# The norm's row scale laid into the third plain tile of each FFN of a one-layer decoder block

## The chip, the cores and the metric

The kernel runs on one core of one Trainium2 chip. The metric is the device time of one execution in microseconds (us); the median of 3 runs is 1043.48 us, the lowest 1042.58 and the highest 1044.74. Engine names are those of the profile: PE does the matmuls and PEld their weight loads, DVE and ACT the elementwise work, POOL hardly anything here, SP issues the loads from HBM.

## What is computed

One layer of a decoder for 512 tokens of width 1024, in float32. The change touches the two feed-forward halves (FFN), which stand before and after the mixing part:

```python
def rms_norm(x, g):
    xf = x.astype(jnp.float32)
    y = xf * lax.rsqrt(jnp.mean(xf * xf, axis=-1, keepdims=True) + EPS)
    return (y * g.astype(jnp.float32)).astype(x.dtype)

def swiglu(x, w_gate, w_up, w_down):
    return (jax.nn.silu(x @ w_gate) * (x @ w_up)) @ w_down
...
        h = h + 0.5 * swiglu(rms_norm(h, ln_ffn1[i]), w1_gate[i], w1_up[i], w1_down[i])
        u = rms_norm(h, ln_mix[i]) @ w_in[i]
...
        h = h + 0.5 * swiglu(rms_norm(h, ln_ffn2[i]), w2_gate[i], w2_up[i], w2_down[i])
```

D_MODEL is 1024 and D_FF is 2816, so one FFN has 22 column tiles of 128.

## The kernel before

The activations lie transposed: `h[k]` holds 128 features by 512 tokens, for 8 values of `k`. Every float32 factor is split into a high and a low part, and one product is three matmuls (`mm3`, lines 228 to 230: high by high, high by low, low by high), each 128 x 128 by 512 columns. The norm's row scale (one number per token) isn't applied to the input. The matmuls run on `h` times the gain, and the scale `rb`, which is the same for all features, multiplies the results as they leave PSUM. So the first tiles can be computed before the scale is known, but none can leave PSUM.

`WStream` delivers the weights: SP loads blocks of 128 x 1024 (`wraw`, 512 KB, 7 buffers), ACT makes the high part (`whi`, line 73) and DVE the low part (`wlo`, line 74), with 3 buffers each, up to 3 pieces ahead of PE. A piece is 8 blocks of 128 x 128, that is 24 matmuls. A `whi` buffer is written again when PE has read it for the last time.

In an FFN, `f` counts the column tiles; each has a gate bank `g` (PSUM pool "acc", 3 banks) and an up bank `u` (pool "t", 3 banks), and takes two pieces, 48 matmuls. Tiles 0 and 1 are computed together (`first`, 96 matmuls), then tile 2 (`plain_pair(2)`, the "third plain tile"), and with it all three pairs of banks are full. Then comes the row scale:

- `norm.finish()`: `col_sums` sums the squares over the features by 4 matmuls against a column of ones (line 268, PSUM tile `ss`), and `rsqrt_of` takes the inverse root by 12 small DVE operations of 128 x 4 (lines 247 to 261);
- `row_bcast`: DVE makes a diagonal matrix in a high and a low part (`dg`, lines 275 and 280), PE multiplies them with ones (lines 282 and 283, PSUM tile `rbp`), and ACT copies the result to `rb` (line 346).

`plain_out` empties a tile: DVE `gs = g * rb` (line 368, frees `g`), ACT `silu(gs)` (line 369, which needs its function table loaded), DVE `a = u * gs` (line 371, frees `u`), and the split of `a` (lines 235 and 236). Tile 3 can start when tile 0's `g` is free. After the plain tiles (6 in the first FFN, 4 in the second) the other tiles are computed as Strassen products of 256 columns (`start_pair`, `end_pair`), whose operands `sx` are formed from `h` by ACT and DVE (`Norm.forms`, lines 316 to 320 and 235, 236; the intermediate is `sf`) and from the weights by DVE (`T1` to `T4`, lines 101 to 110, which write `wraw`). Then comes the down projection.

The program isn't run in the order in which it is written: a scheduler sets each engine's queue, by the dependencies and by when it takes operands to be ready, and each engine then works through its queue in order. So the operand forms of tiles far ahead stand between the operations of the row scale, and the order on the engines has to be read from the queues, below.

## Time and profile before

| | |
|---|---|
| median of 3 runs | 1043.48 us (1042.58 to 1044.74) |
| the profiled execution | 1042.88 us |
| its span, first to last instruction | 1041.1 us |
| PE busy | 1016.6 us, 98% of the span |
| DVE busy | 729.3 us, 70% |
| ACT busy | 449.2 us, 43% |
| PE share of the chain that ended last | 96% |
| mean granted clock of PE | 0.987 of full speed |

The span is the profiled execution without what lies before its first and behind its last instruction (1.8 us here). The time of an engine is the sum of its instructions; matmuls overlap, so a matmul that lasts 0.39 us is followed by the next after 0.23 us when PE is dense. The granted clock tells how much of the 2.4 GHz PE was given: 1.00 is 2.4 GHz, 0.50 is 1.2 GHz. A wait is the idle time of an engine before an instruction, put down to what ended it.

### The profile page before, as it was taken

What the parts mean: (1) busy time and instruction counts of PE and PEld (TensorE: products, weight loads), DVE (VectorE), ACT (ScalarE), POOL (GpSimd) and SP (SyncE); (2) the same over time, 40 slices, a digit from 0 to 9 for tenths busy, and PEclk for the clock granted to TensorE, in tenths of its full rate; (3) what the DMA queues carried; (4) which work ended last, traced back from release to release, by engine and by line L of the source; (5) the groups of instructions that cost most, each with busy time, mean ns of one, the idle gap of its engine ahead of it and who ended that gap; (6) DMA issues with size and microseconds to landing.
All of it is one profiled execution on the core that took longest, in us unless ns stands there. A gap on an engine that the chain in (4) does not pass through costs nothing.

```text
span 1041.1 us, 14828 instructions
## 1 busy us (share of the span) xinstructions
PE 1016.6 (98%) x5987; PEld 886.6 (85%) x5987; DVE 729.3 (70%) x1181; ACT 449.2 (43%) x692; POOL 2.5 (0%) x9
## 2 busy tenths in 40 slices
PE   9799999999999999999999998899999999999996
PEld 7689998899998888887767787799988999988885
DVE  7857975579976668765647676688744698866655
ACT  8334552145544342345443442455522255543443
POOL 0000000000000000000000000000000000000000
PEclk9899999999999999999999999899999999999998
DMA  8212253123343221122210222033333132342301
GB/s 326 61 61 82 82 173 108 61 82 102 111 151 123 92 92 61 51 82 92 72 60 1 82 82 81 5 113 121 122 107 101 61 102 82 133 151 101 101 21 61
DMA packets 28980, 97.68 MB, mean 94 GB/s; under 512 B 3456, under 2 KB 3456, under 8 KB 28912
## 3 DMA queue, kind: packets, MB, share of 16 engines
q1 hardware_dynamic: 28752, 96.25, 27.4%
q8 instruction: 47, 0.77, 0.3%
q0 software_dynamic: 160, 0.49, 0.2%
q14 instruction: 21, 0.17, 0.0%
HBM read 94.10 MB, written 2.10 MB: 92 GB/s over the span
## 4 chain that ended last, share of the span: by engine, by line
PE 96%; DVE 2%; DMA 1%; issue 0%; ACT 0%; SPq 0%; DVEq 0%
PE down L228 8%; PE down L229 8%; PE down L230 8%; PE a L384 6%; PE a L383 6%; PE a L382 6%; PE gu L228 4%; PE gu L229 4%; PE gu L230 4%; PE c L382 3%; PE c L384 3%; PE c L383 3%; PE b L384 2%; PE b L382 2%; PE b L383 2%; PE ufq L228 2%
## 5 line engine op out<-in xcount | busy, mean ns | idle before, releaser
L73 ACT ACTIVATE whi<-wraw 128x1024 fp32r<-128x1024 f32 (+1 forms) x220 | 230.1, 1046 | 394.9 <-PE down L229 94.6
L74 DVE TENSOR_TENSOR wlo<-wraw,whi 128x1024 fp32r<-128x1024 f32 (+1 forms) x220 | 265.1, 1205 | 91.8 <-ACT whi L73 91.0
L228 PE MATMUL down<-ah,whi 128*128 128x512 f32 x352 | 137.1, 390 | 0.0
L229 PE MATMUL down<-al,whi 128*128 128x512 f32 x352 | 137.1, 390 | 0.0
L230 PE MATMUL down<-ah,wlo 128*128 128x512 f32 x352 | 137.0, 389 | 0.0
L382 PE MATMUL c<-sx,whi 128*128 128x256 f32 x272 | 78.7, 289 | 0.9 <-DVE u L416 0.9
L228 PEld LDWEIGHTS down<-ah,whi 128*128 128x128 f32 x352 | 66.1, 188 | 14.1 <-ACT ah L235 0.7
L230 PEld LDWEIGHTS down<-ah,wlo 128*128 128x128 f32 x352 | 66.1, 188 | 13.8
L229 PEld LDWEIGHTS down<-al,whi 128*128 128x128 f32 x352 | 66.1, 188 | 13.7 <-DVE al L236 0.4
L384 PE MATMUL a<-x,wlo 128*128 128x256 f32 x272 | 77.0, 283 | 0.0
L384 PE MATMUL a<-sx,wlo 128*128 128x256 f32 x272 | 77.0, 283 | 0.0
L383 PE MATMUL a<-sx,whi 128*128 128x256 f32 x272 | 77.0, 283 | 0.0
L383 PE MATMUL a<-x,whi 128*128 128x256 f32 x272 | 77.0, 283 | 0.0
L382 PE MATMUL a<-sx,whi 128*128 128x256 f32 x272 | 77.0, 283 | 0.0
L384 PE MATMUL c<-sx,wlo 128*128 128x256 f32 x272 | 77.0, 283 | 0.0
L383 PE MATMUL c<-sx,whi 128*128 128x256 f32 x272 | 76.9, 283 | 0.0
L382 PE MATMUL a<-x,whi 128*128 128x256 f32 x272 | 76.9, 283 | 0.0
L228 PE MATMUL gu<-x,whi 128*128 128x512 f32 x160 | 64.5, 405 | 3.0 <-DVE gs L368 2.8
L229 PE MATMUL gu<-x,whi 128*128 128x512 f32 x160 | 63.9, 401 | 0.0
L230 PE MATMUL gu<-x,wlo 128*128 128x512 f32 x160 | 63.5, 398 | 0.0
L382 PEld LDWEIGHTS c<-sx,whi 128*128 128x128 f32 x272 | 52.1, 191 | 3.5 <-DVE u L416 2.9
L382 PEld LDWEIGHTS a<-sx,whi 128*128 128x128 f32 x272 | 52.2, 192 | 0.1
(306 smaller groups left out, 2173.4 us busy)
## 6 DMA issues: line engine op xcount, KB each, us to landing
wraw<-wst SPq DMA_DIRECT2D x169, 512.0 KB, 3.4
h<-xT SPq DMA_DIRECT2D x8, 256.0 KB, 6.4
out<-y SPq DMA_DIRECT2D x8, 256.0 KB, 2.2
wraw<-wst SPq DMA_DIRECT2D x7, 256.0 KB, 2.6
rpb<-rpa SPq DMA_DIRECT2D x8, 64.0 KB, 2.1
praw<-pT SPq DMA_DIRECT2D x2, 256.0 KB, 3.3
gf<-lnf SPq DMA_DIRECT2D x2, 256.0 KB, 4.3
posi<-pos POOLq DMA_DIRECT2D x1, 256.0 KB, 4.4
```

The lines of the kernel that those rows point to most:

```text
L73: self.nc.scalar.activation(hi, src, AF.Copy)
L74: self.nc.vector.tensor_tensor(lo, src, hi.bitcast(F32), op=ALU.subtract)
L228: PE.matmul(out, a[0], b[0], start=start, stop=False)
L229: PE.matmul(out, a[0], b[1], start=False, stop=False)
L230: PE.matmul(out, a[1], b[0], start=False, stop=stop)
L382: PE.matmul(o, hi[:, c], x[0], start=begin and i == 0 and k == 0, stop=False, skip_group_check=True)
L383: PE.matmul(o, hi[:, c], x[1], start=False, stop=False, skip_group_check=True)
L384: PE.matmul(o, lo[:, c], x[0], start=False, stop=end and i == 1 and k == 3, skip_group_check=True)
```

## The change

The tile's loop becomes a generator that can stop after every second `k`. The column sums are issued in front of tile 2, then a one-element Silu (whose result nobody reads), then three quarters of tile 2 (36 matmuls), then `row_bcast`, then the last quarter. The later plain tiles run as before (`next(plain_tile())` runs all 8 `k`). No operation is left out; two Silu of 128 x 1 are added, one for each FFN.

```diff
--- before.py
+++ after.py
@@ -447,20 +447,27 @@
                     mm3(u, W.next(), norm.x(k), k == MO[0], k == MO[-1])
         g, u = acc("gu"), tps("gu")
 
-        def plain_pair(f):
-            for k in MO:
+        def plain_tile(n=KD):
+
+            for i, k in enumerate(MO):
                 for o in (g, u):
                     mm3(o, W.next(), norm.x(k), k == MO[0], k == MO[-1])
-
-        plain_pair(2)
+                if i % n == n - 1:
+                    yield
+
+        tile2 = plain_tile(2)
         r = norm.finish()
+        S.activation(warm, ones, AF.Silu)
+        for _ in range(3):
+            next(tile2)
         rb = row_bcast(r, "rb")
+        next(tile2)
         for f in range(2):
             plain_out(f, first[2 * f], first[2 * f + 1])
         forms = list(range(4))
         for f in range(2, 2 * n_plain):
             if f > 2:
-                plain_pair(f)
+                next(plain_tile())
             if forms:
                 norm.forms(forms.pop(0))
             if n_plain == 2:
```

What stands in the queues now, at the places on which the prediction rests. Lines up to 449 keep their numbers, those behind the changed piece are 7 higher after. Names carry running numbers: `gu_22` and `gu_23` are `g` and `u` of tile 2 in the first FFN, `gu_51` and `gu_52` those of tile 3, `whi5` and `whi6` tile 2's two pieces.

PE in the first FFN before, from the end of tile 2 to the start of tile 3:

```order
L228 MATMUL gu_23_292<-x_13_253,whi6_301 128x512
L229 MATMUL gu_23_292<-x_13_253,whi6_301 128x512
L230 MATMUL gu_23_292<-x_13_253,wlo6_302 128x512
L268 MATMUL ss_24_365<-ones_96,ssum_14_268 128x1 x4
L282 MATMUL rbp_31_393<-dg_29_386,ones_r_98 128x512
L283 MATMUL rbp_31_393<-dg_30_387,ones_r_98 128x512
L228 MATMUL gu_51_440<-x_6_126,whi7_307 128x512
L229 MATMUL gu_51_440<-x_6_126,whi7_307 128x512
```

PE there after, at the end of tiles 0 and 1 (`gu_5` is tile 1's `u`):

```order
L228 MATMUL gu_5_125<-x_13_253,whi4_237 128x512
L229 MATMUL gu_5_125<-x_13_253,whi4_237 128x512
L230 MATMUL gu_5_125<-x_13_253,wlo4_238 128x512
L268 MATMUL ss_24_293<-ones_96,ssum_14_268 128x1 x4
L228 MATMUL gu_22_291<-x_6_126,whi5_317 128x512
L229 MATMUL gu_22_291<-x_6_126,whi5_317 128x512
L230 MATMUL gu_22_291<-x_6_126,wlo5_318 128x512
```

and further on, from the 38th matmul of tile 2 nearly to its end:

```order
L229 MATMUL gu_22_291<-x_12_232,whi6_323 128x512
L282 MATMUL rbp_31_382<-dg_29_375,ones_r_98 128x512
L230 MATMUL gu_22_291<-x_12_232,wlo6_324 128x512
L228 MATMUL gu_23_292<-x_12_232,whi6_323 128x512
L229 MATMUL gu_23_292<-x_12_232,whi6_323 128x512
L230 MATMUL gu_23_292<-x_12_232,wlo6_324 128x512
L228 MATMUL gu_22_291<-x_13_253,whi6_323 128x512
L229 MATMUL gu_22_291<-x_13_253,whi6_323 128x512
L230 MATMUL gu_22_291<-x_13_253,wlo6_324 128x512
L228 MATMUL gu_23_292<-x_13_253,whi6_323 128x512
L229 MATMUL gu_23_292<-x_13_253,whi6_323 128x512
L283 MATMUL rbp_31_382<-dg_30_376,ones_r_98 128x512
```

The column sums went ahead of tile 2's 48 matmuls; the two broadcast matmuls went into it, the first behind 38 of them and the second behind 47, so that one matmul is left behind it before tile 3. In tile 3 the 12 matmuls of its first half that write `g` still stand ahead of those that write `u`.

DVE in the first FFN before, from the last operand forms to the gate of tile 0 (the rows left out between the two pieces are five more small operations of the inverse root):

```order
L101 TENSOR_TENSOR wraw15_618<-wraw13_614,wraw14_616 128x1024
L319 SCALAR_TENSOR_TENSOR sf_78_677<-h3_74,vec_70,a21_77_676 128x256
L320 SCALAR_TENSOR_TENSOR sf_78_677<-h7_78,vec_70,sf_78_677 128x256
L247 TENSOR_SCALAR rv_25_370<-ss_24_365 128x4
L250 TENSOR_SCALAR ry_26_372<-rv_25_370 128x4
L251 TENSOR_SCALAR ry_26_372<-ry_26_372 128x4
L254 SCALAR_TENSOR_TENSOR rg_28_376<-ry_26_372,rv_25_370 128x4
L256 TENSOR_TENSOR ru_27_375<-rg_28_376,ry_26_372 128x4
L74 TENSOR_TENSOR wlo9_445<-wraw9_442,whi9_444 128x1024
```

```order
L256 TENSOR_TENSOR ru_27_375<-rg_28_376,ry_26_372 128x4
L257 SCALAR_TENSOR_TENSOR ry_26_372<-ru_27_375,ry_26_372 128x4
L275 TENSOR_TENSOR dg_29_386<-ident_112,ry_26_372 128x512
L280 SCALAR_TENSOR_TENSOR dg_30_387<-ident_112,ry_26_372,dg_29_386 128x128 x4
L368 TENSOR_TENSOR gs_33_398<-gu_2_122,rb_32_396 128x512
```

DVE there after, the start of the row scale:

```order
L236 TENSOR_TENSOR sx_56_511<-sf_54_504,sx_55_510 128x512
L247 TENSOR_SCALAR rv_25_298<-ss_24_293 128x4
L250 TENSOR_SCALAR ry_26_300<-rv_25_298 128x4
L74 TENSOR_TENSOR wlo7_330<-wraw7_327,whi7_329 128x1024
L251 TENSOR_SCALAR ry_26_300<-ry_26_300 128x4
L236 TENSOR_TENSOR sx_58_515<-sf_54_504,sx_57_514 128x512
L254 SCALAR_TENSOR_TENSOR rg_28_304<-ry_26_300,rv_25_298 128x4
L317 SCALAR_TENSOR_TENSOR sf_66_590<-h6_77,vec_70,a21_65_589 128x256
L256 TENSOR_TENSOR ru_27_303<-rg_28_304,ry_26_300 128x4
L319 SCALAR_TENSOR_TENSOR sf_66_590<-h2_73,vec_70,a21_65_589 128x256
L257 SCALAR_TENSOR_TENSOR ry_26_300<-ru_27_303,ry_26_300 128x4
L259 SCALAR_TENSOR_TENSOR rg_28_304<-ru_27_303,rg_28_304 128x4
```

and its end, up to the gate of tile 0:

```order
L236 TENSOR_TENSOR sx_70_601<-sf_66_590,sx_69_600 128x512
L257 SCALAR_TENSOR_TENSOR ry_26_300<-ru_27_303,ry_26_300 128x4
L317 SCALAR_TENSOR_TENSOR sf_78_678<-h7_78,vec_70,a21_77_677 128x256
L74 TENSOR_TENSOR wlo8_360<-wraw8_357,whi8_359 128x1024
L275 TENSOR_TENSOR dg_29_375<-ident_112,ry_26_300 128x512
L101 TENSOR_TENSOR wraw15_619<-wraw13_615,wraw14_617 128x1024
L280 SCALAR_TENSOR_TENSOR dg_30_376<-ident_112,ry_26_300,dg_29_375 128x128 x4
L318 SCALAR_TENSOR_TENSOR sf_78_678<-h3_74,vneg_120,sf_78_678 128x256
L319 SCALAR_TENSOR_TENSOR sf_78_678<-h3_74,vec_70,a21_77_677 128x256
L320 SCALAR_TENSOR_TENSOR sf_78_678<-h7_78,vec_70,sf_78_678 128x256
L74 TENSOR_TENSOR wlo9_446<-wraw9_443,whi9_445 128x1024
L368 TENSOR_TENSOR gs_33_399<-gu_2_122,rb_32_385 128x512
```

The small operations of the inverse root, which stood in a row behind all operand forms, now stand one by one between them, and the low diagonal (line 280) comes behind a weight form (line 101); tile 0's gate (line 368) now comes behind `wlo9`, as it did.

PE in the second FFN after, three quarters into tile 2 (`gu_598` and `gu_599` are its `g` and `u`):

```order
L228 MATMUL gu_599_5678<-x_586_5471,whi128_5649 128x512
L229 MATMUL gu_599_5678<-x_586_5471,whi128_5649 128x512
L230 MATMUL gu_599_5678<-x_586_5471,wlo128_5650 128x512
L282 MATMUL rbp_607_5756<-dg_605_5749,ones_r_98 128x512
L283 MATMUL rbp_607_5756<-dg_606_5750,ones_r_98 128x512
L228 MATMUL gu_598_5677<-x_589_5509,whi128_5649 128x512
L229 MATMUL gu_598_5677<-x_589_5509,whi128_5649 128x512
L230 MATMUL gu_598_5677<-x_589_5509,wlo128_5650 128x512
```

DVE in the second FFN before, from the last operand form to the gate of tile 0:

```order
L236 TENSOR_TENSOR sx_646_5919<-sf_642_5908,sx_645_5918 128x512
L107 TENSOR_TENSOR wraw115_5830<-wraw119_5963,wraw115_5830 128x1024
L74 TENSOR_TENSOR wlo129_5681<-wraw113_5678,whi129_5680 128x1024
L74 TENSOR_TENSOR wlo130_5711<-wraw114_5708,whi130_5710 128x1024
L247 TENSOR_SCALAR rv_601_5743<-ss_600_5738 128x4
L250 TENSOR_SCALAR ry_602_5745<-rv_601_5743 128x4
L251 TENSOR_SCALAR ry_602_5745<-ry_602_5745 128x4
L254 SCALAR_TENSOR_TENSOR rg_604_5749<-ry_602_5745,rv_601_5743 128x4
```

DVE there after, the start of the same stretch:

```order
L236 TENSOR_TENSOR sx_646_5921<-sf_642_5910,sx_645_5920 128x512
L247 TENSOR_SCALAR rv_601_5684<-ss_600_5679 128x4
L107 TENSOR_TENSOR wraw115_5832<-wraw119_5965,wraw115_5832 128x1024
L250 TENSOR_SCALAR ry_602_5686<-rv_601_5684 128x4
L74 TENSOR_TENSOR wlo129_5704<-wraw113_5701,whi129_5703 128x1024
L251 TENSOR_SCALAR ry_602_5686<-ry_602_5686 128x4
L254 SCALAR_TENSOR_TENSOR rg_604_5690<-ry_602_5686,rv_601_5684 128x4
L256 TENSOR_TENSOR ru_603_5689<-rg_604_5690,ry_602_5686 128x4
```

and its end:

```order
L257 SCALAR_TENSOR_TENSOR ry_602_5686<-ru_603_5689,ry_602_5686 128x4
L275 TENSOR_TENSOR dg_605_5749<-ident_112,ry_602_5686 128x512
L280 SCALAR_TENSOR_TENSOR dg_606_5750<-ident_112,ry_602_5686,dg_605_5749 128x128 x4
L74 TENSOR_TENSOR wlo130_5734<-wraw114_5731,whi130_5733 128x1024
L368 TENSOR_TENSOR gs_609_5773<-gu_594_5553,rb_608_5759 128x512
```

Here both broadcast matmuls stand behind 36 of tile 2's 48, with 12 behind them. On DVE the inverse root went ahead of `wlo130` and `wlo131`, and a weight form that waits for a load (line 107) stands between its first two operations.

ACT at the start of the program, after:

```order
L213 ACT_TABLE_LOAD
L213 ACTIVATE warm_110<-ones_96 128x1
L460 ACTIVATE warm_110<-ones_96 128x1 x2
L543 ACT_TABLE_LOAD
L543 ACTIVATE lbe0_1533<-lbe0_1533 128x4
L238 ACTIVATE x_6_126<-h0_71,vec_70 128x512
```

Both added Silu (line 460) stand here and not at the FFNs, since they need nothing but `ones`: in both FFNs the order on ACT is still `rb`, table load, `gs`, as in this piece of the second FFN after:

```order
L73 ACTIVATE whi129_5703<-wraw113_5701 128x1024
L73 ACTIVATE whi130_5733<-wraw114_5731 128x1024
L346 ACTIVATE rb_608_5759<-rbp_607_5756 128x512
L369 ACT_TABLE_LOAD
L369 ACTIVATE gs_609_5773<-gs_609_5773 128x512
L73 ACTIVATE whi131_5838<-wraw117_5836 128x1024
```

There `whi131`, which stood ahead of `rb`, went behind the first Silu. The order of the loads on SP and of the work on POOL is the same in both kernels.

## Rows read from the trace of the kernel before

**Rows 1.** The page: busy us, share, instructions; the chain that ended last.
```profile
PE 1016.6 (98%) x5987; PEld 886.6 (85%) x5987; DVE 729.3 (70%) x1181; ACT 449.2 (43%) x692; POOL 2.5 (0%) x9
...
PE 96%; DVE 2%; DMA 1%; issue 0%; ACT 0%; SPq 0%; DVEq 0%
```

**Rows 2.** Who PE waited for: total us, times, longest us.
```profile
PE rbp L282 <- DVE dg L275: 9.4, 2, 5.2
PE gu L228 <- DVE gs L368: 2.8, 2, 1.4
```

**Rows 3.** Timeline of PE, first FFN: start, duration, instruction, [idle before].
```profile
28.34 0.39 PE L228 MATMUL gu<-x,whi 128*128 128x512 f32 x1
...
39.22 0.95 PE L268 MATMUL ss<-ones,ssum 128*128 128x1 f32 x8
44.39 0.77 PE L282 MATMUL rbp<-dg,ones_r 128*128 128x512 f32 x1 [4.22 <-DVE dg L275]
...
47.68 0.79 PE L228 MATMUL gu<-x,whi 128*128 128x512 f32 x1 [1.41 <-DVE gs L368]
...
52.42 0.39 PE L228 MATMUL gu<-x,whi 128*128 128x512 f32 x1
```

**Rows 4.** Timeline of DVE, first FFN.
```profile
29.63 0.69 DVE L236 TENSOR_TENSOR sx<-sf,sx 128x512 fp32r<-128x512 f32 x1 [0.24 <-ACT sx L235]
30.58 1.23 DVE L74 TENSOR_TENSOR wlo<-wraw,whi 128x1024 fp32r<-128x1024 f32 x1 [0.26 <-ACT whi L73]
31.72 0.69 DVE L236 TENSOR_TENSOR sx<-sf,sx 128x512 fp32r<-128x512 f32 x1
32.44 0.48 DVE L317 SCALAR_TENSOR_TENSOR sf<-h,vec,a 128x256 f32<-128x256 f32 x1
...
41.01 0.16 DVE L256 TENSOR_TENSOR ru<-rg,ry 128x4 f32<-128x4 f32 x1
41.09 1.23 DVE L74 TENSOR_TENSOR wlo<-wraw,whi 128x1024 fp32r<-128x1024 f32 x1
...
42.50 0.16 DVE L256 TENSOR_TENSOR ru<-rg,ry 128x4 f32<-128x4 f32 x1
42.70 0.16 DVE L257 SCALAR_TENSOR_TENSOR ry<-ru,ry 128x4 f32<-128x4 f32 x1
...
43.55 0.69 DVE L275 TENSOR_TENSOR dg<-ident,ry 128x512 fp32r<-128x512 f32 x1
44.28 1.14 DVE L280 SCALAR_TENSOR_TENSOR dg<-ident,ry,dg 128x128 fp32r<-128x128 f32 x4
46.93 0.69 DVE L368 TENSOR_TENSOR gs<-gu,rb 128x512 f32<-128x512 f32 x1 [1.51 <-ACT rb L346]
```

**Rows 5.** Timeline of ACT, first FFN.
```profile
39.24 1.06 ACT L73 ACTIVATE whi<-wraw 128x1024 fp32r<-128x1024 f32 x1 [3.39 <-issue]
46.30 0.60 ACT L346 ACTIVATE rb<-rbp 128x512 f32<-128x512 f32 x1 [6.00 <-PE rbp L283]
46.92 1.28 ACT L369 ACT_TABLE_LOAD   x1
48.21 0.63 ACT L369 ACTIVATE gs<-gs 128x512 f32<-128x512 f32 x1
```

**Rows 6.** Timeline of PE, second FFN.
```profile
646.05 0.95 PE L268 MATMUL ss<-ones,ssum 128*128 128x1 f32 x8
655.44 0.80 PE L228 MATMUL gu<-x,whi 128*128 128x512 f32 x1 [1.41 <-DVE gs L368]
...
659.40 0.40 PE L228 MATMUL gu<-x,whi 128*128 128x512 f32 x1
```

**Rows 7.** Timeline of DVE, second FFN.
```profile
636.00 1.23 DVE L107 TENSOR_TENSOR wraw<-wraw,wraw 128x1024 f32<-128x1024 f32 x1 [2.20 <-DMA wraw<-wst]
```

**Rows 8.** Windows: length; PE, PEld, DVE, ACT, POOL busy; granted clock; DMA.
```profile
41.50:42.00 0.50, 0.00 (x0) 0.00 (x0) 0.50 (x1) 0.00 (x0) 0.00 (x0) 0.53 0.00 0
```

**Rows 9.** Timeline of ACT, start of the program.
```profile
4.04 0.72 ACT L238 ACTIVATE x<-h,vec 128x512 fp32r<-128x512 f32 x1 [0.29 <-DMA h<-xT]
```

## The prediction, made before the changed kernel was run

> **What bounds the kernel now.** I read the page first: PE is busy for 98% of the span and is 96% of the chain that ended last [rows 1], so a change counts by what it does to PE's idle time and to PE's clock. Next, whom PE waited for: nearly all of it is two waits, 9.4 us in total for the diagonal `dg` and 2.8 us for tile 0's gate, each twice, that is once in each FFN [rows 2]. Then the timelines of the two places. In the first FFN PE ends tile 2, does the column sums at 39.22, stands idle for 4.22 us until `dg` is there, does the two broadcasts, waits 1.41 us more for the gate and starts tile 3 at 47.68 [rows 3]; in the second FFN the sums start at 646.05 and tile 3 at 655.44 [rows 6]. What fills that time is one chain: sums, inverse root, diagonal (DVE), broadcast (PE), copy (ACT), gate (DVE) [rows 3 to 5]. Last the clock: in the first FFN PE's clock fell in the window from 41.5 us, during the idle time [rows 8], to half, and came back only during tile 3. At full clock a matmul of 512 columns takes 0.227 us (48 of tile 2 from 28.34 to 39.22 are 10.88) [rows 3]; tile 3's first 13 took 4.74 us, from 47.68 to 52.42, and not 2.95, which is 1.8 us lost. In the second FFN the first 9 took 3.96, from 655.44 to 659.40, and not 2.04: 1.9 us lost [rows 6].
>
> **Moved: the sums.** They take 0.95 us before and after [rows 3, 6]; they stand ahead of tile 2 and not behind it. Nothing gained by itself. What is queued behind them is tile 2, and the squares that they wait for are summed long before (the operand forms that follow these sums on DVE are under way at 29.63 [rows 4]).
>
> **First FFN, the inverse root and the diagonal.** The sums now run from 28.34 to 29.29. DVE's first small operation follows the `sx` of 29.63, at 30.25. Up to the high diagonal DVE has 12 small operations and, between them, two `wlo`, three `sx` and five `sf` that belong to later tiles. An operation overlaps the next by 0.09 (30.58 + 1.23 against 31.72), so a `wlo` costs 1.14, an `sx` 0.60, an `sf` 0.40 [rows 4]: 2.28 + 1.80 + 2.00 = 6.1 us. A small operation costs 0.20 where the next one needs its result (42.50 to 42.70) and 0.08 where it doesn't (41.01 to 41.09) [rows 4]; in the new order only two of the twelve are followed at once by one that needs them, so 2 x 0.20 + 10 x 0.08 = 1.2. With 0.1 for the wait of the first `wlo` for its high part (30.58) the high diagonal starts at 30.25 + 6.1 + 1.2 + 0.1 = 37.65 and ends at 38.34. Its broadcast starts 0.15 later, as at 43.55 + 0.69 against 44.39 [rows 3, 4]: 38.5. PE gets there after 38 matmuls, at 29.29 + 8.62 = 37.9. So PE waits 0.6 us in the middle of tile 2, a new wait, with the last ten matmuls behind it. The low diagonal follows a weight form of 1.14 and takes 1.14 itself [rows 4]: 40.55. PE needs it after the broadcast and 9 matmuls, at 38.5 + 2.27 = 40.76. No wait.
>
> **First FFN, what is late next.** ACT has to make `whi9` before it copies `rb`, and `whi9` needs the buffer that PE reads until the 47th matmul, which starts at 40.53 and ends 0.39 later, at 40.92 [rows 3]. It starts 0.08 later, as at 39.24 [rows 5], and `rb` 0.97 after that, at 42.0; with 0.63 from `rb` to the gate (46.30 to 46.93 [rows 4, 5]) the gate could start at 42.6. But `wlo9` stands ahead of it on DVE, waits for `whi9` and runs from 42.1 to 43.24. The gate takes 0.75 until PE starts (46.93 to 47.68 [rows 3, 4]): tile 3 starts at 43.99, after 2.6 us of idle PE, against 47.68: **3.7 us gained**. If each small operation costs 0.20 all of it shifts by 1.2 and 2.5 are gained; without the 0.6 us wait 4.3 are.
>
> **The clock there.** No row of before shows a single idle time of PE between 1.4 and 4.2 us. The lower bound of the loss is none; the upper is what tile 3 lost before, 1.8 us. I take the upper one: the clock fell at 41.5 at the earliest 1.3 us after PE had stopped at 40.17 [rows 3, 8], half of the idle time that I expect. So the 1.8 us stay as they are and none is gained.
>
> **Second FFN.** Tile 2 started at 646.05 - 10.88 = 635.17, so the sums now end at 636.12. On DVE the first small operation runs, then line 107, which waited for a load until 636.00 [rows 7] and is ready; with 1.14 for it and 1.14 for `wlo129`, then ten small operations in a row at 0.20 or less, the high diagonal starts at 640.5, and the low one ends at 640.5 + 0.73 + 1.14 = 642.4 [rows 4]. PE gets to the broadcasts after 36 matmuls, at 636.12 + 8.16 = 644.3, so 1.9 us are to spare. `rb` is copied from 645.0 to 645.6 and the gate ends at 646.3; PE has two broadcasts and 12 matmuls left, 14 x 0.227 = 3.2, and ends tile 2 at 647.5. So tile 3 starts without a wait, at 647.5 against 655.44, 8.0 us, and with no idle time the 1.9 us of slow clock go too: **9.9 us gained**.
>
> **The second bank.** Tile 3's `u` needs the Silu. The added Silu of the change stand at the head of ACT's queue, so each FFN still loads the table behind `rb`. In the rows the load of 1.28 us is followed at once by the Silu, 46.92 to 48.21 [rows 5]. With 0.63 for it and 0.69 for `a`, `u` is free 3.3 us after `rb` starts: at 45.3 in the first FFN, where PE asks for it 13 matmuls into tile 3 at 46.9, and at 648.3 in the second, 7 matmuls in, at 649.1. No wait, by 1.6 and 0.8 us. The Trainium skill (ScalarE: Activation LUTs, "What ACT_TABLE_LOAD costs") puts a drain of about 1.38 us behind each load; the rows have none, and by the page the second FFN would wait 0.6 us.
>
> **Added and not on the path.** The two Silu of 128 x 1 at the start cost 0.2 us each; ACT had 0.29 us idle there before its first `x` [rows 9], so 0.15 us is left, which I add in full. The loads on SP keep their order, and by the time that PE runs ahead the loads of the next pieces have landed: DVE's and ACT's waits there are for PE. I cost them at nothing; if that cover fails, PE waits for DVE's weight forms.
>
> **The sum.** 3.7 + 9.9 - 0.15 = 13.45 us off 1042.88 is 1029.4 for an execution like the profiled one. The median lies 0.6 above that one: **1030.0**.
>
> **Rivals.**
> - *The clock holds in the first FFN.* Then 1.8 us more, 1028.2. For it: 2.6 us idle is less than the 4.2 us that showed the fall. Chance 0.30.
> - *The first FFN only trades its wait.* If the forms between the small operations run later than their durations say (they wait for ACT's `sx`, as at 29.63), PE stands in the middle of tile 2 for what it stood for behind it. Gain of the first FFN 0 to 2.5: 1031.2 to 1033.7. Chance 0.12.
> - *The table load drains.* If the Silu starts later than the rows show, as by the page above, 0.6 us in the second FFN: 1030.6. The rows speak against it. Chance 0.05.
> - *Given back later.* PE arrives 9.9 us earlier at the Strassen products, and DVE has to empty three tiles and make the weight forms for them in the time of tile 3. Three times four operations of 0.60, three `wlo` and two forms of 1.14 are 12.9 us, against 10.9 of tile 3 and 3.2 of the last quarter: it just fits. ACT's Silu between them could stretch it; what doesn't fit comes back as waits for weight forms, at worst in both FFNs and all of it: 1030 to 1043. Chance 0.05, of which 0.03 within 0.2%.
> - *Slower.* In the second FFN line 107 stands ahead of the inverse root and waits for a load; it already waited 2.20 us [rows 7]. Each us that the load is late beyond the 1.9 to spare stops PE in tile 2 for 1 us. From 13.45 + 1.9 = 15.4 us late the kernel is slower; at 20 us it would take 1048. Nothing in the rows has a load that late. Chance 0.02.
> - *The change doesn't do what it says.* That is so for the table load and is in the sum; a hoisted load would have brought nothing, since PE doesn't wait for `u`.
>
> **Chances and range.** The forecast has 0.46. The range 1027.0 to 1033.0 holds it, the clock that holds with 1 us of error, the page's rule and most of the traded wait, about 0.85. A measurement can tell about 0.2% of this kernel, 2.1 us, from no change. Faster by more: 0.95; within: 0.03; slower: 0.02.
>
> **What would show it.** Right: in the second FFN no wait of PE from tile 2 to tile 3 and a granted clock of 1.00 throughout; in the first a wait before the first broadcast of about 0.6 us and one of about 2.6 us before tile 3, put down to the gate, with `wlo9` just ahead of the gate on DVE; a table load behind `rb` in both. Wrong: a wait before the broadcasts in the second FFN, a wait for `u` inside tile 3, or new waits of PE in the products behind the plain tiles.

## The result, and the profile after

The changed kernel takes 1028.76 us, the median of 4 runs (1027.57 to 1029.40), against 1043.84 for the kernel before, timed beside it (4 runs): a ratio of 0.9855, with a 95% interval of 0.9838 to 0.9872. The profiled execution took 1029.4 us, of which 1027.6 are its span. The forecast was 1030.0, and 1029.4 for a profiled execution.

The page of the changed kernel, to be read against [rows 1]: busy us, share, instructions by engine, then the chain that ended last.

```profile
PE 1011.9 (98%) x5987; PEld 883.5 (86%) x5987; DVE 727.4 (71%) x1181; ACT 449.4 (44%) x694; POOL 2.5 (0%) x9
...
PE 93%; DVE 3%; issue 1%; DMA 1%; ACT 1%; SPq 0%; DVEq 0%; ACTq 0%
```

PE is busy for 4.7 us less with the same number of matmuls. So about a third of the 13.5 us is not idle time of PE. By the rows below, about half of that third is tile 3, which ran at the lower clock for a shorter time in the first FFN (0.28 us) and not at all in the second (1.93 us). The rest is mostly the broadcasts: before, these four matmuls lasted 0.77 to 0.80 us each (the first is in [rows 3]), alone and at the lower clock; now they stand among others, where one matmul follows the next after 0.23 to 0.32 us. Whom PE waited for (total us, times, longest us), against [rows 2]:

```profile
PE gu L228 <- DVE gs L368: 2.6, 1, 2.6
...
PE gu L228 <- ACT whi L73: 0.9, 1, 0.9
PE rbp L282 <- DVE dg L275: 0.4, 1, 0.4
```

The 9.4 us for the diagonal have shrunk to 0.4, and the gate's 2.8 us in two waits are now one wait of 2.6 us. The first FFN shows where these two are. First PE from the start of tile 2 to that of tile 3, against [rows 3] (start, duration, instruction, [idle before]):

```profile
28.20 0.95 PE L268 MATMUL ss<-ones,ssum 128*128 128x1 f32 x8
...
37.53 0.39 PE L229 MATMUL gu<-x,whi 128*128 128x512 f32 x1
38.34 0.47 PE L282 MATMUL rbp<-dg,ones_r 128*128 128x512 f32 x1 [0.42 <-DVE dg L275]
...
40.72 0.39 PE L283 MATMUL rbp<-dg,ones_r 128*128 128x512 f32 x1
...
43.94 0.50 PE L228 MATMUL gu<-x,whi 128*128 128x512 f32 x1 [2.59 <-DVE gs L368]
```

Then DVE in the same stretch, against [rows 4], and ACT, against [rows 5]:

```profile
37.51 0.69 DVE L275 TENSOR_TENSOR dg<-ident,ry 128x512 fp32r<-128x512 f32 x1
38.11 1.22 DVE L101 TENSOR_TENSOR wraw<-wraw,wraw 128x1024 f32<-128x1024 f32 x1
39.25 1.14 DVE L280 SCALAR_TENSOR_TENSOR dg<-ident,ry,dg 128x128 fp32r<-128x128 f32 x4
...
42.06 1.23 DVE L74 TENSOR_TENSOR wlo<-wraw,whi 128x1024 fp32r<-128x1024 f32 x1 [0.49 <-ACT whi L73]
43.20 0.68 DVE L368 TENSOR_TENSOR gs<-gu,rb 128x512 f32<-128x512 f32 x1
44.59 0.69 DVE L371 TENSOR_TENSOR a<-gu,gs 128x512 f32<-128x512 f32 x1 [0.70 <-ACT gs L369]
```

```profile
40.97 1.06 ACT L73 ACTIVATE whi<-wraw 128x1024 fp32r<-128x1024 f32 x1 [4.97 <-issue]
41.94 0.58 ACT L346 ACTIVATE rb<-rbp 128x512 f32<-128x512 f32 x1
42.53 1.28 ACT L369 ACT_TABLE_LOAD   x1
43.92 0.63 ACT L369 ACTIVATE gs<-gs 128x512 f32<-128x512 f32 x1
```

The sums now stand ahead of tile 2, at 28.20. The high diagonal starts at 37.51, PE waits 0.42 us for it in the middle of tile 2 (counted from the end of the matmul of 37.53; the broadcast fell due 0.23 us after that matmul's start, at 37.76, and came 0.58 us later), and the low broadcast at 40.72 waits for nothing. ACT makes `whi9` at 40.97 and copies `rb` only behind it; DVE makes `wlo9` at 42.06, behind a wait for `whi9`, and only then the gate at 43.20. For that PE stands idle for 2.59 us and starts tile 3 at 43.94. The granted clock in windows there (length; PE, PEld, DVE, ACT, POOL busy; granted clock; DMA share, GB/s), against [rows 8]:

```profile
44.00:44.50 0.50, 0.50 (x2) 0.42 (x3) 0.00 (x0) 0.50 (x1) 0.00 (x0) 1.00 0.61 66
45.00:45.50 0.50, 0.50 (x4) 0.36 (x3) 0.50 (x2) 0.19 (x1) 0.00 (x0) 0.82 0.81 311
46.00:46.50 0.50, 0.50 (x3) 0.40 (x2) 0.50 (x1) 0.50 (x1) 0.00 (x0) 0.50 0.51 205
49.00:49.50 0.50, 0.50 (x3) 0.39 (x3) 0.50 (x1) 0.00 (x0) 0.00 (x0) 1.00 0.00 0
```

The clock falls to half, from 2.4 to 1.2 GHz, but not in the idle time: PE ended tile 2 at 43.94 - 2.59 = 41.35 and was back at work at 43.94, and the clock stood at 1.00 until 45.0. It is back at 1.00 in the window at 49.0. In the second FFN, PE and DVE, against [rows 6] and [rows 7]:

```profile
631.83 0.95 PE L268 MATMUL ss<-ones,ssum 128*128 128x1 f32 x8
...
640.95 0.39 PE L282 MATMUL rbp<-dg,ones_r 128*128 128x512 f32 x1
641.18 0.39 PE L283 MATMUL rbp<-dg,ones_r 128*128 128x512 f32 x1
...
644.14 0.39 PE L228 MATMUL gu<-x,whi 128*128 128x512 f32 x1
```

```profile
632.81 0.16 DVE L247 TENSOR_SCALAR rv<-ss 128x4 f32<-128x4 f32 x1 [2.35 <-PE ss L268]
632.89 1.22 DVE L107 TENSOR_TENSOR wraw<-wraw,wraw 128x1024 f32<-128x1024 f32 x1
...
637.08 0.69 DVE L275 TENSOR_TENSOR dg<-ident,ry 128x512 fp32r<-128x512 f32 x1
...
642.24 0.69 DVE L368 TENSOR_TENSOR gs<-gu,rb 128x512 f32<-128x512 f32 x1 [1.67 <-ACT rb L346]
```

No row of PE there has an idle time, the granted clock is 1.00 in every half microsecond from 630 to 662, and line 107, which waited 2.20 us for its load before, waits for nothing. The gate at 642.24 waited for the copy `rb`, and is done 1.2 us before PE, with sums, 48 matmuls and two broadcasts behind it, reaches tile 3 at 644.14.

For the balance I take the gate of tile 3, which waits for that tile's last matmul, as the end of each FFN's plain part. The four rows, the kernel before first (DVE, line 368):

```profile
60.10 0.69 DVE L368 TENSOR_TENSOR gs<-gu,rb 128x512 f32<-128x512 f32 x1 [2.07 <-PE gu L230]
...
667.77 0.69 DVE L368 TENSOR_TENSOR gs<-gu,rb 128x512 f32<-128x512 f32 x1 [0.93 <-PE gu L230]
```

```profile
56.08 0.69 DVE L368 TENSOR_TENSOR gs<-gu,rb 128x512 f32<-128x512 f32 x1 [1.84 <-PE gu L230]
...
654.54 0.69 DVE L368 TENSOR_TENSOR gs<-gu,rb 128x512 f32<-128x512 f32 x1 [0.93 <-PE gu L230]
```

| stretch | before, us | after, us | difference |
|---|---|---|---|
| start of the program to tile 2 (after: the sums ahead of it), first FFN | 28.34 | 28.20 | -0.14 |
| to the gate of tile 3, first FFN | 31.76 | 27.88 | -3.88 |
| to the start of tile 2, second FFN (635.17 before, 631.83 after) | 575.07 | 575.75 | +0.68 |
| to the gate of tile 3, second FFN | 32.60 | 22.71 | -9.89 |
| to the end of the span | 373.33 | 373.06 | -0.27 |
| span | 1041.1 | 1027.6 | -13.5 |

### The profile page after: what moved, and what is told of

Its sections match the earlier page's. It is cut to its first block, busy times and chain, and to the rows that moved or that the text cites. A ratio compares the mean times of both kernels' runs of the same rounds, so it can differ in the third digit from the quotient of the medians.

```text
span 1027.6 us, 14828 instructions
## 1 busy us (share of the span) xinstructions
PE 1011.9 (98%) x5987; PEld 883.5 (86%) x5987; DVE 727.4 (71%) x1181; ACT 449.4 (44%) x694; POOL 2.5 (0%) x9
## 4 chain that ended last, share of the span: by engine, by line
PE 93%; DVE 3%; issue 1%; DMA 1%; ACT 1%; SPq 0%; DVEq 0%; ACTq 0%
PE down L228 8%; PE down L229 8%; PE down L230 8%; PE a L384 6%; PE a L383 6%; PE a L382 6%; PE c L382 3%; PE c L383 3%; PE c L384 3%; PE gu L228 3%; PE gu L230 3%; PE gu L229 3%; PE b L384 2%; PE b L383 2%; PE b L382 2%; PE ufq L228 2%
## 5 line engine op out<-in xcount | busy, mean ns | idle before, releaser
L228 PE MATMUL gu<-x,whi 128*128 128x512 f32 x160 | 63.0, 397 | 3.5 <-DVE gs L368 2.6
L229 PE MATMUL gu<-x,whi 128*128 128x512 f32 x160 | 62.6, 392 | 0.0
```

Of the source, the lines that this page charges most:

```text
L228: PE.matmul(out, a[0], b[0], start=start, stop=False)
L229: PE.matmul(out, a[0], b[1], start=False, stop=False)
```

## Experiments

Each kernel differs from the changed kernel by the diff shown. The two with the change in one FFN, the one with the broadcast behind tile 2 and the one with the table load hoisted ran on one chip beside 9 runs of the kernel before (median 1043.17). The one without the small Silu and the one with the broadcast at half of tile 2 ran on another (7 runs, 1042.94), the other four on a third (9 runs, 1043.14). Ratios are to these.

**The change in the first FFN alone, and in the second alone.** `n_plain` is 3 in the first FFN and 2 in the second; the other FFN keeps the old order.

```diff
-        r = norm.finish()
-        S.activation(warm, ones, AF.Silu)
-        for _ in range(3):
+        early = n_plain == 3
+        for _ in range(0 if early else 4):
             next(tile2)
+        r = norm.finish()
+        if early:
+            S.activation(warm, ones, AF.Silu)
+            for _ in range(3):
+                next(tile2)
         rb = row_bcast(r, "rb")
-        next(tile2)
+        if early:
+            next(tile2)
```

> The change in the first FFN alone; the second FFN as in the kernel before. My theory, that the two FFNs add up and the first one only shortens its wait: tile 3 starts at about 43.9 instead of 47.68, PE still idle about 2.6 us before it, the clock falls in most runs; 3.5 us off the median of before (1043.8), so 1040.3, and about 1.8 less in runs in which the clock holds. In the second FFN the old waits (5.2, 0.3, 1.4 us) stand as before. Rival, that the first FFN's gain is given back in the products behind the plain tiles (0.7 us of it was in the profiled execution of the changed kernel): 1041 to 1043.

> The change in the second FFN alone. My theory: all of its idle time and its slow clock go, 9.9 us, so 1033.9 from 1043.8, with no PE wait between tile 2 and tile 3 of the second FFN and the old waits (4.2, 0.3, 1.4 us) in the first. Rival, that the second FFN's gain needs what the first one moved (loads or operand forms that arrive earlier): less than 8 us, above 1036.

Measured: the first FFN alone 1037.24 us, ratio 0.9947 (0.9934 to 0.9961); the second alone 1032.46 (for it, `early = n_plain == 2`), ratio 0.9900 (0.9887 to 0.9914). The second FFN's part brought 10.7 us, 0.8 more than its term; in its profile the stretch from tile 2 to the gate of tile 3 in that FFN is 22.72 us (635.74 to 658.46), 9.88 less than before, as the term has it. The first FFN's brought 5.9, 2.2 more than its term of 3.7, and its 1037.24 us is met neither by the theory (1040.3, or 1.8 less where the clock holds) nor by the rival (1041 to 1043). Its profiled execution shows where most of that comes from; PE and the gate of tile 3, and the clock where the changed kernel's had fallen:

```profile
37.90 0.47 PE L282 MATMUL rbp<-dg,ones_r 128*128 128x512 f32 x1 [0.41 <-DVE dg L275]
...
43.49 0.50 PE L228 MATMUL gu<-x,whi 128*128 128x512 f32 x1 [2.59 <-DVE gs L368]
```

```profile
54.02 0.69 DVE L368 TENSOR_TENSOR gs<-gu,rb 128x512 f32<-128x512 f32 x1 [1.84 <-PE gu L230]
```

```profile
45.00:45.50 0.50, 0.50 (x4) 0.42 (x3) 0.42 (x1) 0.50 (x2) 0.00 (x0) 1.00 0.77 303
46.00:46.50 0.50, 0.50 (x4) 0.42 (x3) 0.50 (x2) 0.09 (x1) 0.00 (x0) 1.00 0.07 25
```

The wait of 2.59 us is the same to the hundredth, but the clock stood at 1.00 behind it, and from tile 3's start to its gate it took 54.02 - 43.49 = 10.53 us where the changed kernel took 56.08 - 43.94 = 12.14. So one and the same idle time is followed by a fall of the clock in one execution and not in another, and the fall costs 1.6 us. The two parts alone make 16.6 us, both together 15.1 (15.4 in the later four runs); I have no reading that accounts for all of that 1.2 to 1.5 us. The fall of the clock, which comes in some executions and not in others, is of that size, and so is the interval of each of these gains, 1.4 to 1.8 us either way.

**The sums in front, the broadcast behind the whole tile 2.** The other half of the change is undone.

```diff
-        for _ in range(3):
+        for _ in range(4):
             next(tile2)
         rb = row_bcast(r, "rb")
-        next(tile2)
```

> The column sums in front of tile 2 in both FFNs, but the broadcast behind the whole tile, not at three quarters. Theory: in the first FFN the place of the broadcast is worth nothing, since the diagonal and the high part of the next weights are late either way: tile 3 starts at about 43.7, as with the change (43.94) or 0.3 earlier. In the second FFN the last quarter no longer covers copy and gate, and the next high part stands ahead of the copy on ACT: PE idle 2 to 3 us before tile 3 and the clock may fall: 3 to 5 us slower than the changed kernel (1028.8), so 1031.5 to 1033.8. Rival, that the sums in front are the whole gain: 1028.8.

Measured: 1030.77 us, ratio 0.9878 (0.9862 to 0.9894), 0.7 below the theory's span. Tile 3's start in the first FFN and in the second:

```profile
43.19 0.50 PE L228 MATMUL gu<-x,whi 128*128 128x512 f32 x1 [2.43 <-DVE gs L368]
...
645.35 0.80 PE L228 MATMUL gu<-x,whi 128*128 128x512 f32 x1 [2.32 <-DVE gs L368]
```

and ACT in the first FFN:

```profile
40.05 1.06 ACT L73 ACTIVATE whi<-wraw 128x1024 fp32r<-128x1024 f32 x1 [4.22 <-issue]
```

In the second FFN tile 3 now waits 2.32 us, and its first matmul is already a slow one, 0.80 us: from the start of tile 2 to the gate it took 26.88 us (630.57 to 657.45), 4.2 more than in the changed kernel. So in this execution, the slowest of its four, the early broadcast is worth that much in the second FFN, 1.7 us of it for the lower clock in tile 3 (12.10 us to the gate, against 10.40 in the changed kernel). It isn't worth as much in each run: the medians differ by 2.0 us, and one of the four took 1027.59 us with a mean clock of 0.998, as fast as the fastest of the changed kernel's first four.

In the first FFN the early broadcast is worth less than nothing: tile 3 starts 15.00 us after the sums (28.19), against 15.74 in the changed kernel and 15.18 to 15.75 in the five other profiled executions with the broadcast at three quarters. The rows point to why. `whi9` starts 0.08 to 0.09 us after the end of tile 2's 47th matmul in the kernel before, in the changed kernel and here, as the prediction read it: that matmul frees its buffer. With the change, the first broadcast and the wait for it stand ahead of that matmul and hold it up by 0.9 us (the broadcast fell due at 37.76, the matmul behind it starts at 38.66); so `whi9` starts at 40.97 there and at 40.05 here, with `rb` and the gate behind it.

**The table load hoisted for good.** The small Silu now reads the inverse root, so it can't go to the head of ACT's queue.

```diff
-        S.activation(warm, ones, AF.Silu)
+        S.activation(warm, r[:, :1], AF.Silu)
```

> The changed kernel with the added Silu reading the inverse root instead of the ones, so that it can't be placed at the start: the table load stands ahead of the broadcast's copy in both FFNs. Theory: PE waits for the gate, not for the Silu, so nothing is gained: 1028.8 within 1 us; the first Silu follows the gate without a load and tile 0's second bank is free 0.7 to 1.3 us earlier. Rival, that the load behind the copy still costs PE time (the second bank, or the load's drain): 1.3 us for each FFN, 1026.2.

Measured: 1028.49 us, ratio 0.9859 (0.9845 to 0.9872), as the theory had it. The load stands ahead of `rb` in both FFNs, and the wait before tile 3 in the first is 2.59 us all the same: PE waits for the gate's multiply, which doesn't need the table. In the first FFN the load behind `rb` had been hidden: the Silu starts 0.72 us after the gate's multiply with it (43.20 to 43.92) and without it (42.18 to 42.90). The 0.7 to 1.3 us that I expected for tile 0's second bank came only in the second FFN, as 0.55 (1.27 us there in the changed kernel, 0.72 here). In this profiled execution the clock held too (42.92 to a gate at 53.45 is 10.53 us).

**The line with the small Silu left out.**

```diff
-        S.activation(warm, ones, AF.Silu)
```

> The changed kernel without its line with the one-column Silu between the column sums and the second plain tile. Both executions of that line stand at the program's start (2.27, 0.44 us for the two), on ScalarE ahead of the first operand form, and the table load of the first gate stands behind the copy rb all the same. Theory of the prediction: the first form starts 0.1 to 0.2 us earlier and nothing else moves, so 0.15 us less, which this measurement can't tell from none: 1027.5 to 1028.6. Rival: the line does keep a table or a state of ScalarE that the first gate needs, and without it the first gate comes late and TensorE's 2.6 us of idle grow: more than 1029.5.

Measured: 1028.51 us, ratio 0.9868 (0.9851 to 0.9884). ACT's first operand form starts at 3.97 us instead of 4.13, and the sums ahead of tile 2 at 28.07 instead of 28.20. With the line, the sums ahead of tile 2 started anywhere from 27.76 to 28.26 in the profiled executions of the kernels with that order, so what the line costs is lost in that spread. No help and no harm of the line can be told from these times.

**The changed kernel again, and its idle time filled.** The fill is 11 matmuls that nobody reads.

```diff
         next(tile2)
+        if n_plain == 3:
+            idle = aux("idle")
+            for i in range(11):
+                PE.matmul(idle, ones_r, norm.x(MO[0])[0], start=(i == 0), stop=(i == 10))
```

> The changed kernel once more, on the chip of the three runs that follow, so that they are read against it. Its first four runs lay at 1027.6 to 1029.4 us, granted clock 0.995 three times and 0.998 once. Theory: TensorE stands idle for 2.6 us ahead of the third plain tile of the first FFN, and only in some executions does the clock fall behind that gap, which costs about 1.6 us; so five more runs should fall into two groups, around 1027 with a clock near 0.998 and around 1028.7 with one near 0.995. Rival: the spread has nothing to do with that gap, and the times lie evenly.

> The changed kernel with 11 matmuls added that nobody reads (128x512, 0.22 us each, 2.4 us together), in the first FFN between the last matmul of the second plain tile and the first of the third, into the bank of the column sums. They fill the 2.6 us in which TensorE waits for VectorE's gate, and move nothing on any other engine. Theory: the third tile starts at the same time, 43.9, and the only thing that goes is the fall of the clock that follows the gap: no run has a clock of 0.995, all lie near 1027.2, that is 1.6 us below the changed kernel's disturbed runs. Rival one: the clock has nothing to do with the gap and the time stays at 1028.7. Rival two: the filler runs at the lower clock or past the gate and the time rises by up to 2.4 us, to 1031.

Measured: the changed kernel again 1027.73 us (1026.66 to 1028.48), ratio 0.9855 (0.9841 to 0.9868); with the fill 1027.12 (1026.05 to 1028.04), ratio 0.9849 (0.9836 to 0.9863). The times alone don't tell the two apart, and they don't fall into two groups: with the fill they spread as widely. The traces do. PE with the fill, tile 3's gate, and the clock:

```profile
40.77 2.72 PE L468 MATMUL idle<-x,ones_r 128*128 128x512 f32 x11
43.53 0.50 PE L228 MATMUL gu<-x,whi 128*128 128x512 f32 x1
```

```profile
54.05 0.69 DVE L368 TENSOR_TENSOR gs<-gu,rb 128x512 f32<-128x512 f32 x1 [1.84 <-PE gu L230]
```

```profile
45.00:45.50 0.50, 0.50 (x4) 0.41 (x3) 0.47 (x1) 0.50 (x2) 0.00 (x0) 1.00 0.95 393
46.00:46.50 0.50, 0.50 (x4) 0.42 (x3) 0.50 (x2) 0.13 (x1) 0.00 (x0) 1.00 0.00 0
```

Tile 3 starts when it did, and from there to its gate it takes 10.52 us, against 12.15 in the changed kernel's second profiled execution, on the same chip (43.41 to 55.56). The mean clock of the runs agrees: without the fill, 9 of 12 runs (the changed kernel twice, and the one without the small Silu) have 0.995 or 0.996, and so have 3 of 4 with the table load hoisted, where the gap is the same. With the fill all 4 have 0.997 or 0.998, and so have all 13 runs of the three kernels below, which have no such gap. So the idle time does bring the fall, though not in every execution, and the theory's 1.6 us hold for one fall; that the spread of the times is this fall and nothing else is wrong.

**The broadcast at a higher priority; the inverse root too; the broadcast at half of tile 2.** Three ways to get the copy and the gate past the weight forms of `whi9` and `wlo9`. In the second the inverse root has the priority as well:

```diff
-        r = norm.finish()
+        with tc.high_priority():
+            r = norm.finish()
...
-        rb = row_bcast(r, "rb")
+        with tc.high_priority():
+            rb = row_bcast(r, "rb")
```

and in the first only the lower of these two edits is made. In the third the numbers alone change:

```diff
-        for _ in range(3):
+        for _ in range(2):
             next(tile2)
         rb = row_bcast(r, "rb")
-        next(tile2)
+        for _ in range(2):
+            next(tile2)
```

> The changed kernel with the broadcast (diagonal pair, two matmuls, ScalarE's copy) at a higher priority, the inverse root left where it is. In the first FFN VectorE's diagonal then goes ahead of the low form of weight 8 and both diagonals ahead of the sum of weight 15, ScalarE's copy rb ahead of the high form of weight 9, and VectorE's gate ahead of the low form of weight 9. From rows of the changed kernel: high diagonal 1.2 us earlier, rb at the end of the high form of weight 8, about 41.0 instead of 41.94, gate at about 41.6 instead of 43.2, third tile at about 42.2 instead of 43.94, so TensorE's 2.6 us of idle shrink to 0.9. Theory (the copy and the gate stood behind weight forms that nobody needed yet): 1.7 us less, and where the shorter gap lets the clock stand, 1.6 us less again in the disturbed runs: 1025.5 to 1027.0 against the changed kernel's 1028.7. Rival: what the first FFN wins is given back at the first Strassen pairs, since the forms of weights 8 and 9 and the sum of weight 15 come later: 1028.7 or more.

> The changed kernel with the inverse root and the broadcast both at a higher priority: the column sums go inside the tiles ahead of the second plain tile, the 13 small operations of the inverse root run between VectorE's operand forms as they come due, both broadcast matmuls are issued in the first third of the second plain tile, and the gate of the first tile is done long before the third one needs its bank. Theory (all of what is left ahead of the third tile in the first FFN is order on VectorE and ScalarE, not work that TensorE must wait for): the 2.6 and 0.4 us of wait go, with them the clock's fall of 1.6 us where there is one: about 1024 to 1025.7. Rival one: the operand forms of the Strassen products are pushed back by as much and TensorE waits for them at the first pair: 1027 to 1029. Rival two: the column sums now wait for VectorE's sum of squares in the midst of the first tiles, in TensorE's own queue, and cost more than is won: above 1029.

> The changed kernel with the broadcast written behind two quarters of the second plain tile instead of three (in both FFNs). In the first FFN the planner then puts the high diagonal ahead of the low form of weight 8, both diagonals ahead of the sum of weight 15, the copy rb ahead of the high form of weight 9 and the gate ahead of the low form of weight 9, as the run with the broadcast at a higher priority did; the high broadcast moves 7 matmuls up in TensorE's queue, to about 34.9, while the high diagonal ends at about 36.5. Theory (order on VectorE and ScalarE is what made TensorE idle ahead of the third tile): TensorE now waits about 1.6 us for the high diagonal, and then not at all, or under 0.3 us, ahead of the third tile, which starts at about 42.2 instead of 43.4 to 43.9; the wait is too short or too early to matter otherwise, and the clock stands: 1025.5 to 1027. Rival: a quarter of a tile is what the diagonal needs, so the wait only changes its place and the clock falls as before: 1028 to 1029.

Measured: the broadcast alone 1025.43 us, ratio 0.9834 (0.9820 to 0.9847), and with the inverse root 1024.44, ratio 0.9824 (0.9811 to 0.9837), both on the chip where the changed kernel took 1027.73; at half 1025.07, ratio 0.9835 (0.9821 to 0.9850), against 1028.51 for the kernel without the small Silu on the same chip. The second lies inside its theory's span, the first and the third 0.1 and 0.4 us below theirs. Of the one with the broadcast at half, PE, then ACT and DVE:

```profile
28.26 0.94 PE L268 MATMUL ss<-ones,ssum 128*128 128x1 f32 x8
...
37.27 0.47 PE L282 MATMUL rbp<-dg,ones_r 128*128 128x512 f32 x1 [0.41 <-DVE dg L275]
...
39.66 0.39 PE L283 MATMUL rbp<-dg,ones_r 128*128 128x512 f32 x1
...
41.05 0.40 PE L230 MATMUL gu<-x,wlo 128*128 128x512 f32 x1
41.50 0.50 PE L228 MATMUL gu<-x,whi 128*128 128x512 f32 x1
```

```profile
40.09 0.60 ACT L346 ACTIVATE rb<-rbp 128x512 f32<-128x512 f32 x1 [4.02 <-PE rbp L283]
41.30 1.06 ACT L73 ACTIVATE whi<-wraw 128x1024 fp32r<-128x1024 f32 x1 [0.61 <-PE gu L229]
```

```profile
36.44 0.68 DVE L275 TENSOR_TENSOR dg<-ident,ry 128x512 fp32r<-128x512 f32 x1
...
40.75 0.69 DVE L368 TENSOR_TENSOR gs<-gu,rb 128x512 f32<-128x512 f32 x1
...
42.39 1.23 DVE L74 TENSOR_TENSOR wlo<-wraw,whi 128x1024 fp32r<-128x1024 f32 x1 [0.16 <-ACT whi L73]
```

The copy now stands ahead of `whi9` and the gate ahead of `wlo9`. Tile 2's last matmul ends at 41.45 and tile 3 starts at 41.50, so PE's idle time before tile 3 went from 2.59 us to 0.05. Tile 3 starts 13.24 us after the sums instead of 15.74, and the granted clock stays at 1.00.

The order of the two weight forms is not all of that. In the trace the broadcast stands behind 33 matmuls of tile 2 and not behind 38, so the low broadcast too starts sooner, 11.40 us after the sums (39.66) instead of 12.52 (40.72). The gate comes 2.5 us sooner after the sums (12.49 us against 15.00). Here `rb` starts 0.43 us after the low broadcast and the gate 0.66 after `rb`; with these steps the changed kernel's gate could have started at 41.81 instead of 43.20. So, as an estimate, 1.4 us are the two weight forms and 1.1 the earlier broadcast; no run parts the two.

The wait that I expected in the midst of tile 2, 1.6 us, is 0.41. Both times behind it were slips: the broadcast moved up by 5 matmuls and not 7 and fell due at 36.7, not at 34.9, and the high diagonal ended at 37.12, not at 36.5. With the broadcast alone at a higher priority the queue is nearly the same: again 33 matmuls stand ahead of the broadcast, and tile 3 starts 13.20 us after the sums, with no idle time in the profile where I had expected 0.9 us. With the inverse root at a higher priority, the gate is done long before PE asks, and tile 3's gate comes at

```profile
51.52 0.69 DVE L368 TENSOR_TENSOR gs<-gu,rb 128x512 f32<-128x512 f32 x1 [2.27 <-PE gu L230]
```

51.52, 4.6 us earlier than in the changed kernel, and PE's longest wait up to there, behind the start of the program, is 0.5 us, ahead of the sums (23.04), for DVE's sum of squares, which the second rival had named. Of the kernels here this is the fastest, 3.3 us less than the changed kernel on the same chip. What it wins in the first FFN reaches the end only in part: its span is 3.1 us below that of the changed kernel on that chip, where the gate was 4.0 earlier (51.52 against 55.56).

## Why the prediction was right, point by point

- **The sums moved.** Right: 0.95 us before and after, with nothing waiting.
- **First FFN, inverse root and diagonal.** The sum of small operations and forms gave a high diagonal at 37.65; it came at 37.51, and from the start of tile 2, which was 0.14 earlier, just as foreseen. The new wait of 0.6 us, forecast from the time at which the broadcast falls due, is 0.58 so counted, 0.42 of it idle in the profile; it is no fixed sum, though: 0.25 in the changed kernel's second profiled execution, and 0.01 without the small Silu. No wait for the low diagonal: right.
- **First FFN, what is late next.** `whi9`, `rb`, `wlo9`, gate, in that order, 2.6 us of idle PE (2.59 measured), tile 3 at 43.99 (43.94). The term of 3.7 us measured 3.88 to the gate of tile 3, of which 0.3 is a shorter stretch at the lower clock (12.42 us from tile 3's start to its gate before, 12.14 after). This was the step that mattered most. It also names what was left to win, and the runs with the broadcast at half and at a higher priority took it, with an earlier broadcast besides.
- **The clock.** The result was right for the profiled execution, the reason was not. I argued that the clock would fall inside the idle time, 1.3 us after PE stops, as before. It fell more than 1 us after PE had come back (1.00 until 45.0, 0.82 on average in the half microsecond from there), and in two of the five profiled executions with the 2.59 us wait (the first FFN alone, the table load) it didn't fall at all. So the choice between 1.8 us lost and none, which I treated as one answer to be found, is drawn anew in each execution; the rival with 0.30, the clock that holds, came true in some runs. What decides it no run here shows. The price was sized fairly: 1.6 us measured, against 1.8. The 1.8 counts 13 matmuls between 47.68 and 52.42, where the trace has 12, so the loss there was 2.0; to the gate of tile 3 it was 1.9 (12.42 us against 10.53).
- **Second FFN.** 9.9 us forecast, 9.89 measured, in the two parts that the sum has: 7.96 us to the start of tile 3, and 1.93 from there to its gate (12.33 before, 10.40 after), where the clock now stays up. The high diagonal was put 5.3 us behind the start of tile 2 and came 5.25 behind it (637.08 - 631.83); line 107 waited for no load, which ended the rival on the slower side.
- **The second bank.** Right. The Trainium skill (ScalarE: Activation LUTs, "What ACT_TABLE_LOAD costs") puts a drain of about 1.38 us behind a load. The trace doesn't agree here: the load of 42.53 ends at 43.81, the gate's multiply at 43.88, and the Silu starts at 43.92. The run with the load hoisted, 1028.49 us, agrees that no wait of PE hung on it.
- **The small Silu.** 0.15 us was added for it; ACT's first form started 0.09 us later than before (4.13 against 4.04) and 0.16 later than without the line, but the first FFN's tile 2, or the sums ahead of it, started 0.14 earlier than before. The run without the line gained nothing. A term of this size was below what one execution differs from the next at the start.
- **The first FFN only trades its wait.** It did so in small: 0.58 us in the middle of tile 2. The run with the broadcast behind tile 2 starts tile 3 0.74 us sooner after the sums, since there neither that wait nor the first broadcast (0.3 us) holds up `whi9`.
- **Given back later.** I had 0.05 for it and nothing in the sum, and I put the loads at nothing. The stretch between the two FFNs took 0.68 us more in the profiled execution. DVE's line 101 at 100.78 waited 2.17 us for a load, where before it waited 0.70, and one matmul at 119.70 waited 0.23 us for DVE. The other profiles show that the loss goes with this load (512 KB). In seven executions it took 4.9 to 5.2 us from issue to landing, and the stretch took 575.51 to 576.17 us: the changed kernel twice, without the small Silu, the first FFN alone, the table load hoisted, the broadcast at half and alone at a higher priority. In four it took at most 3.5 us, and the stretch 575.07 to 575.21: the kernel before, the second FFN alone, the broadcast behind tile 2 and the fill. So the cover of the loads, which the prediction named as a condition, failed by 0.4 to 1.1 us in those seven. It isn't simply the price of being early: with the fill and with the first FFN alone tile 3's gate came at the same time (54.05 and 54.02), and the stretch took 575.16 and 576.00 us. Why the load lands late stays open.
- **The median.** I put the median 0.6 us above the profiled execution, as for the kernel before; here the profiled one was the slowest of its four, 0.64 above the median. That difference is the whole miss: 1029.4 was forecast and measured for a profiled execution, and the median is 1028.76 and not 1030.0. That the profiled execution came out at the forecast to a tenth is in part luck: the 0.68 us given back were made up for by the 0.18 us that the first FFN brought beyond its term, by 0.14 at the start and 0.27 at the end, which no term foresaw, and by the 0.15 added for the Silu; and in an execution in which the clock holds it would have been 1.6 us less.

## What to carry to other kernels

When a chain of small operations is laid beside a big engine's work, follow it through every queue to the point where its result is used: here the gain of the first FFN was cut by about 1.4 us (an estimate) by one weight form on ScalarE and one on VectorE that nobody needed yet. A broadcast written one quarter of a tile earlier, or put at a higher priority, was issued sooner, passed both forms and brought 2.3 to 3.4 us more, the clock that then held included. The quickest check on such a sum is a stretch table, from one row that marks the start to one that marks the end of each stage, since it shows both terms and what is given back between them. Terms below what the start of the program varies by from one execution to the next (0.5 us here) can be left out of the sum and kept in the range.

## What the runs showed that I had not expected

An idle time of TensorE of 2.59 us, the same to the hundredth, was followed by a stretch at the lower clock in three profiled executions (the changed kernel twice, and without the small Silu) and by none in two (first FFN alone, table load hoisted). Where it came, it began after the engine was at work again and not while it stood idle, and cost 1.6 us. With the broadcast behind tile 2, gaps of 2.43 and 2.32 us in one execution were followed by it too, the second just as the engine came back (the granted clock is 0.77 on average from 645.0 to 645.5, and the tile starts at 645.35). Filling the idle time with work that nobody reads kept the clock up in that profile at no other cost that the trace shows, but the median moved by only 0.6 us, inside the spread of the runs.
